# NSA's values and window keys projected beside the stick-breaking values in a two-layer decoder trunk

## The chip, the cores and the metric

The kernel runs on one core of one Trainium2 chip. The metric is the device time of one execution in microseconds. Five engines work on their own in-order queues: TensorE (PE, matmuls, with its weight load PEld), VectorE (DVE), ScalarE (ACT), GpSimd (POOL) and SyncE (SP), which issues nearly all transfers here.

## The reference

Two layers over 512 tokens of width 1024. Each layer normalises its input, projects it once with `w_in`, feeds five attention branches from the columns of that product, gates and merges their outputs, projects them and adds the residual:

```python
h = _rmsnorm(x, norm_g)
p = _split_columns(h @ w_in)
...
y_a = _dsa_attention(q_a, k_a, v_a, qi, ki, p['idx_w'])        # A: top-128 keys by an indexer
y_b = _fox_attention(...)                                      # B: forgetting attention
y_c = _stick_breaking_attention(heads(p['sb_q']), heads(p['sb_k']), heads(p['sb_v']))
y_d = _nsa_attention(q_d, _rope(p['nsa_kc'], positions), p['nsa_vc'],
                     _rope(p['nsa_ks'], positions), p['nsa_vs'],
                     _rope(p['nsa_kw'], positions), p['nsa_vw'], gates, ...)
y_e = _memory_attention(heads(p['mem_q']), mem_k, mem_v)       # E: 256 memory tokens
...
merged = jnp.sum(merge * jnp.einsum('bsnc,ncd->bsnd', ys, w_branch), axis=2)
return x + merged @ w_out
```

Each branch has four heads of 64. NSA (branch D) has one 64-wide key and value per token, shared by the heads, for each of three parts: compressed (`kc`, `vc`), selected blocks (`ks`, `vs`) and the local window (`kw`, `vw`). Keys are rotated (`_rope`), values are not. The indexer of branch A picks 128 keys for every query: `lax.top_k(score, 128)`.

## The kernel before

**Products.** Every float32 product is made of three matmuls. Each operand is split in a rounded part (`hi`) and the rest (`lo`), and hi x hi, hi x lo and lo x hi are summed in a PSUM bank (`mm3`, line 264). Weights come in half chunks of 128 x 1024 (512 KB, `load`, line 277): SyncE issues the transfer into `wraw` (two buffers), ScalarE copies it to `whi` (line 271), VectorE subtracts to get `wlo` (line 272); three buffers each. `proj` (line 520) then makes 128 columns of `h @ w_in` for all 512 tokens: eight k tiles of 128 times three matmuls, 24 matmuls of 128x512 into a bank named `pj`. Such an output has its columns on partitions (channel-major). Banks come from three pools: `pj` (3), `S` (2), `T` (3). Intermediate 128x512 tiles come from one pool of `NST` slots.

**The chunks concerned.** `PAIRS` puts two such projections in one weight chunk. Half `('k1', 0)` holds `nsa_kc` and `nsa_ks`; its other half `k2` holds `nsa_kw` in 64 columns and nothing in the others; the second half of `ckv`'s chunk, `v1`, holds `nsa_vs` and `nsa_vw`.

**First stage of a layer** (`first`, from line 711). It works on `u = x * g`, before the norm factor is known, so that it can start early. It projects queries and keys of the first stick-breaking pair (banks `p`), sums squares, and gets the norm factor `y` of each token (`rs_y` in the profile). Then it forms the stick-breaking values for all tokens, token-major: the x tiles are the stationary operand, 256 weight columns move, 4 token blocks x 8 k tiles x 3 = 96 matmuls of 128x256. After two token blocks, `rowb` spreads `y` over the partitions as `rb` (line 364). ScalarE evacuates the values with the factor `y` into `VC` (line 780). `norm` (line 785) forms `hr = x * g * rb` (line 791) and its parts `h_hi`, `h_lo`, on which every later projection waits.

**The later stages of a layer** are built by `weave` (line 675), which draws from several generators in turn by weights; `chain` puts generators behind each other, `take(g, n)` draws only n steps of one. The stages: `sb_attn(0)` (first stick-breaking pair) with side projections; `sb_attn(1)` with more projections and the first two steps of `nsa_proj`; the memory stage, `mem_attn` with `merge(2)`, the rest of `nsa_proj` and 18 steps of `topk`; the NSA stage, `nsa_attn` with `merge(4)`, `dsa_proj` and the rest of `topk`; then DSA, FoX and the last merges, and the output projection. The text drawn so is not the order on the chip: a scheduler places every instruction on its engine's queue by priority and by its own estimate of when inputs are ready. Weight loads and splits get a high priority (`early`).

**nsa_proj** (from line 1090): `k1` is projected and rotated, its upper half becomes the selected keys `KS`; `k2` is projected, rotated and becomes the window keys `KW` (`shared_k`, line 498, writes a key to both halves of a tile with its low part); `v1` is projected, copied out (`vraw`), turned to token-major by four transposes into the bank `vt` (line 1137) and copied to `VSW` (line 1139), whose columns 0-63 of a block are selected values and 64-127 window values.

**topk** (from line 930 on): 16 rounds for each of three blocks of queries (256, 384 and 512 keys wide): VectorE finds the 8 largest (`MAX8`, line 933) and replaces them (`MATCH_REPLACE8`, line 934). 48 such block rounds per layer; each is one step of the generator. Three comparisons (line 937) then make the masks, which only `dsa_attn` reads.

Of the kernel before, what the change touches and what calls it, by code (L numbers as in the profile page):

```python
# [28 lines left out]
NST = 28  # L29
# [18 lines left out]
def _tiles():  # L48
# [19 lines left out]
    k2 = -np.ones(128, int)  # L68
    k2[0:64] = c('nsa_kw', a(64))
    t['k2'] = k2  # L70
    t['v1'] = np.concatenate([c('nsa_vs', a(64)), c('nsa_vw', a(64))])
# [10 lines left out]
PAIRS = [('v2', 'iq'), ('k1', 'k2')]  # L82
PAIRS += [(('sb_q', 0), ('sb_k', 0)), (('sb_q', 1), ('sb_k', 1))]
PAIRS += [('ckv', 'v1'), (('dsa_q', 0), ('dsa_q', 1)), (('nsa_q', 0), ('nsa_q', 1))]
# [3 lines left out]
VTOK = ['sb_v', 'fox_v']  # L88
# [5 lines left out]
for _n in ['memk', 'memv', 'wc1k', 'wc1v'] + [f'wb{n}' for n in range(5)] + [f'wo{n}' for n in range(4)]:  # L94
    CH[_n] = len(CH)
# [8 lines left out]
def _layout(x, mem, positions, norm_g, w_in, kv_norm, w_uk, w_uv, fox_bias, nsa_pe_k, nsa_pe_v,  # L104
# [6 lines left out]
    for l in range(L):  # L111
# [75 lines left out]
def trunk(ctx: ExitStack, tc: tile.TileContext, xt, memt, pos, wall, small, vec, ca, cb, out):  # L187
# [89 lines left out]
    def load(l, key, half):  # L277
        with early():
            r = wts.tile([128, 1024], F32, name="wraw", tag="raw", bufs=2)
            nc.sync.dma_start(r, wall[l, CH[key], :, 1024 * half:1024 * half + 1024])  # L280
        return r

    def wload(l, key, half, r=None):
        r = load(l, key, half) if r is None else r
        with early():
            hi = wts.tile([128, 1024], F32R, name="whi", tag="whi", bufs=3)
            lo = wts.tile([128, 1024], F32R, name="wlo", tag="wlo", bufs=3)
# [420 lines left out]
    def layer(l, xs, begin):  # L708
# [3 lines left out]
        def first():  # L712
# [32 lines left out]
            w = []  # L745
            for half in range(2):
                if l:
                    w.append(wload(l, 'sb_v', half))
                else:
                    r = load(l, 'sb_v', half)  # L750
                    w.append([wts.tile([128, 1024], F32R, name="w", tag=t, bufs=3) for t in ("whi", "wlo")])
                    after(nc.scalar.activation(w[half][0], r, AF.Copy), state['start'][0])
                    after(nc.vector.tensor_sub(w[half][1], r, f32(w[half][0])), state['start'][1])
            lv.VC = wk.tile([128, NB, 256], F32, name="VC", tag="v", bufs=1)
            vb = []
# [16 lines left out]
            yield  # L772
            lv.QC += q_stack(qr)
# [4 lines left out]
            for t in range(2):  # L778
                for e in range(2):
                    nc.scalar.activation(lv.VC[:, 2 * t + e], vb[t][:, e], AF.Copy, scale=y[:, 2 * t + e:2 * t + e + 1])  # L780
# [309 lines left out]
        def nsa_proj():  # L1090
            kr = rope(pj('k1'))
# [374 lines left out]
```

## Time and profile before

| what | value |
|---|---|
| median of 3 runs | 1329.06 us (1328.14 to 1329.29) |
| the profiled execution | 1328.6 us, its span 1326.8 us |
| granted TensorE clock, mean | 0.998 |
| instructions | 18877 |
| busiest engine | PE 1297.0 us, 98% of the span |
| next | DVE 913.9 us, 69%; ACT 677.2 us, 51% |

The span is the time from the first to the last instruction; the execution is 1.8 us longer. The busy time of an engine is the time in which one of its instructions is under way; since matmuls are pipelined, one's duration is longer than the distance to the next. The lines of groups read: line, engine, operation, output<-inputs by tile name, shapes, count, then busy us and mean ns of one, then the idle time just before them and what ended it. In a timeline: start, duration, engine, line, operation, output<-inputs, shapes. In layer 0 the first stage ends at about 36 us, `sb_attn(0)` at 100, `sb_attn(1)` at 162, the memory stage at 255 and the NSA stage near 380.

### The profile page before, as it was taken

To read this page: it belongs to the slowest core of one execution; us is meant where nothing else is said; L and a number is where in the kernel's file an instruction comes from. 1 tells how busy PE (TensorE), PEld (TensorE's weight loads), DVE (VectorE), ACT (ScalarE), POOL (GpSimd) and SP (SyncE) were. 2 spreads that over 40 slices of the span, in tenths; PEclk is the share of its full clock that TensorE was granted. 3 is DMA by queue.
4 is the path that set the end of the run, shared out by engine and by line. 5 is a ranking of instruction groups with operands and counts; after the bars stand their busy time and mean duration, and the time that the engine had idled before them with its cause. 6 is when DMAs were issued, how large, how long until landed. Compare 5 with 4: busy or idle time off the path is not lost.

```text
span 1326.8 us, 18877 instructions
## 1 busy us (share of the span) xinstructions
PE 1297.0 (98%) x7160; PEld 1063.6 (80%) x7160; DVE 913.9 (69%) x1966; ACT 677.2 (51%) x1265; POOL 41.8 (3%) x60
## 2 busy tenths in 40 slices
PE   7999999999999999999999999999999999999997
PEld 6777777888788888888887777877878878888897
DVE  6887999777755556554667699996686564574554
ACT  6887835356544434333447696534584443342341
POOL 0000011000000000000000001110000000000000
PEclk9999999999999999999999999999999999999999
DMA  6432232222213221233623323223122222223231
GB/s 223 137 127 73 90 108 64 82 78 75 72 64 103 67 92 58 70 104 125 192 88 127 96 64 128 80 64 95 49 88 64 79 88 70 91 79 112 96 112 64
DMA packets 40235, 124.10 MB, mean 94 GB/s; under 512 B 4432, under 2 KB 6480, under 8 KB 40144
## 3 DMA queue, kind: packets, MB, share of 16 engines
q1 hardware_dynamic: 40144, 122.89, 28.5%
q8 instruction: 56, 0.92, 0.3%
q14 instruction: 35, 0.29, 0.1%
HBM read 118.16 MB, written 4.72 MB: 93 GB/s over the span
## 4 chain that ended last, share of the span: by engine, by line
PE 70%; DVE 6%; ACT 5%; issue 2%; DMA 1%; POOL 0%; DVEq 0%; ACTq 0%
PE pj L261 59%; PE Y L261 4%; PE S L261 3%; PE pt L573 3%; ACT whi L271 1%; DVE wlo L272 1%; DVE score L934 1%; DVE m L933 1%; ACT sw L448 1%; ACT sw L447 1%; DMA mraw<-in_memt_dram 1%; PE sbz L261 0%; ACT sp_t L405 0%; ACT Qi L877 0%; DVE rt L450 0%
## 5 line engine op out<-in xcount | busy, mean ns | idle before, releaser
L261 PE MATMUL pj<-h_hi,whi 128*128 128x512 f32 x1088 | 431.2, 398 | 1.3 <-DVE rt L450 1.0
L261 PE MATMUL pj<-h_lo,whi 128*128 128x512 f32 x1088 | 428.5, 394 | 0.0
L261 PE MATMUL pj<-h_hi,wlo 128*128 128x512 f32 x1088 | 428.3, 394 | 0.0
L271 ACT ACTIVATE whi<-wraw 128x1024 fp32r<-128x1024 f32 x183 | 193.4, 1057 | 333.0 <-PE pj L261 173.7
L272 DVE TENSOR_TENSOR wlo<-wraw,whi 128x1024 fp32r<-128x1024 f32 x183 | 223.6, 1222 | 185.7 <-ACT whi L271 167.2
L261 PEld LDWEIGHTS pj<-h_hi,wlo 128*128 128x128 f32 x1088 | 204.3, 188 | 46.4 <-DVE wlo L272 3.1
L261 PEld LDWEIGHTS pj<-h_hi,whi 128*128 128x128 f32 x1088 | 204.5, 188 | 42.7 <-DVE rt L450 1.8
L261 PEld LDWEIGHTS pj<-h_lo,whi 128*128 128x128 f32 x1088 | 204.6, 188 | 41.3 <-issue 2.6
L564 ACT ACTIVATE P<-P,nm 128x128 f32<-128x128 f32 (+3 forms) x128 | 71.5, 559 | 77.7 <-DVE nm L563 77.0
L261 PE MATMUL pj<-yhi,whi 128*128 128x512 f32 (+1 forms) x192 | 72.5, 378 | 1.3 <-ACT whi L271 0.5
L563 DVE CUSTOM_DVE_ANT_0 P<-S,CA 128x128 f32<-128x128 f32 (+3 forms) x104 | 48.5, 470 | 35.9 <-PE S L261 35.7
L261 PE MATMUL pj<-ylo,whi 128*128 128x512 f32 (+1 forms) x192 | 71.8, 374 | 0.0
L261 PE MATMUL pj<-yhi,wlo 128*128 128x512 f32 (+1 forms) x192 | 71.7, 374 | 0.0
L573 PE MATMUL pt<-CA,P 128*128 128x128 f32 x384 | 60.2, 274 | 1.7 <-DVE P L612 1.4
L573 PEld LDWEIGHTS pt<-CA,P 128*128 128x128 f32 x384 | 45.6, 141 | 13.0 <-issue 5.0
L411 ACT ACTIVATE G<-pj 128x512 f32<-128x512 f32 x92 | 53.7, 583 | 1.9 <-PE pj L261 1.7
L934 DVE MATCH_REPLACE8 score<-m,score 128x256 f32<-128x256 f32 (+2 forms) x96 | 51.6, 541 | 0.0
L261 PE MATMUL S<-Ks,Qs 128*128 128x256 f32 (+2 forms) x160 | 49.3, 347 | 0.9 <-DVE nm L563 0.9
L933 DVE MAX8 m<-score 128x8 f32<-128x256 f32 (+2 forms) x96 | 49.8, 547 | 0.0
L828 DVE SCALAR_TENSOR_TENSOR G<-G,pj 128x512 f32<-128x512 f32 x64 | 43.6, 681 | 1.3 <-PE pj L261 0.8
L829 DVE TENSOR_TENSOR acc<-acc,G 128x512 f32<-128x512 f32 x64 | 44.0, 687 | 0.7
L261 PEld LDWEIGHTS pj<-yhi,whi 128*128 128x128 f32 x192 | 36.1, 188 | 9.2 <-ACT yhi L271 1.3
(333 smaller groups left out, 2028.2 us busy)
## 6 DMA issues: line engine op xcount, KB each, us to landing
wraw<-in_wall_dram SPq DMA_DIRECT2D x192, 512.0 KB, 3.7
wc<-in_wall_dram SPq DMA_DIRECT2D x16, 256.0 KB, 5.9
x<-in_xt_dram SPq DMA_DIRECT2D x8, 256.0 KB, 5.8
mraw<-in_memt_dram SPq DMA_DIRECT2D x4, 512.0 KB, 4.5
xo<-in_xt_dram SPq DMA_DIRECT2D x8, 256.0 KB, 3.9
xspill<-xn SPq DMA_DIRECT2D x8, 256.0 KB, 2.2
xo<-xspill SPq DMA_DIRECT2D x8, 256.0 KB, 3.0
out_dram<-o SPq DMA_DIRECT2D x8, 256.0 KB, 2.2
```

Source lines behind the costliest of these rows:

```text
L261: return nc.tensor.matmul(out_, lhsT, rhs, start=start, stop=stop, **kw)
L271: nc.scalar.activation(hi, raw, AF.Copy)
L272: nc.vector.tensor_sub(lo, raw, hi.bitcast(F32))
L411: i = nc.scalar.activation(*a, **k)
L447: nc.scalar.activation(sw[a], p[b], AF.Copy)
L563: nc.vector.tensor_tensor_reduce(P, S, mask, -1.0, 3e38, OP.add, OP.min, nm)
L564: nc.scalar.activation(P, P, AF.Exp, bias=nm, scale=-1.0, accum_out=sums)
L573: nc.tensor.transpose(pt[:, 128 * j:128 * j + 128], x[:, c:c + 128], ident)
L828: nc.vector.scalar_tensor_tensor(G, G, gc, p, op0=gop, op1=OP.mult)
L829: nc.vector.tensor_add(acc, acc, G)
L933: nc.vector.max(m8, lv.work[i])
L934: nc.vector.match_replace(lv.work[i], m8, lv.work[i], REPL)
```

## The change

The 192 columns of `nsa_vs`, `nsa_vw` and `nsa_kw` move beside the 256 of the stick-breaking values. The first stage now forms all 448 columns token-major: 96 matmuls of 128x448 in place of 96 of 128x256, from four half chunks of 128x896 (`vt0`, `vt1`) in place of two of 128x1024. The loops are turned: the k tile is outside, the token block inside, so four banks (one of `pj`, both of `S`, one of `T`) are open at once and `rowb` comes after half of the k tiles. `VC` takes 256 columns, a new tile `VK` the other 192, both times `y`. NSA's attention reads its values from `VK` as they lie. The window keys need columns on partitions: a new function `window_keys`, drawn at the end of the side chain of `sb_attn(0)`, transposes columns 64 to 191 of `VK` (four transposes into the bank `kwT`), rotates them and makes `KW`. The projections of `k2` and `v1`, `vraw`, the transposes `vt` and `VSW` are gone; `k1` shares a chunk with `ckv`. Besides, the weave draws 14 block rounds of the top-k in the memory stage, not 18, the weight of the rest in the NSA stage is 40, not 36, the side chain's weight in `sb_attn(0)` is 11, not 10, and `NST` is 27, not 28.

```diff
-NST = 28
+NST = 27
...
-    t['v1'] = np.concatenate([c('nsa_vs', a(64)), c('nsa_vw', a(64))])
+    t['vt'] = np.concatenate([c('sb_v', a(256)), c('nsa_vs', a(64)), c('nsa_vw', a(64)), c('nsa_kw', a(64))])
...
-PAIRS = [('v2', 'iq'), ('k1', 'k2')]
+PAIRS = [('v2', 'iq'), ('ckv', 'k1')]
...
-            w = []
-            for half in range(2):
+            v = [bank("v", t)[:, :448] for t in ("pj", "S", "S", "T")]
+            for i in range(KT // 2):
                 if l:
-                    w.append(wload(l, 'sb_v', half))
+                    hi, lo = wload(l, f'vt{i // 2}', i % 2, n=896)
...
-            for t in range(0, NB, 2):
-                v = bank("pj", "S", (128, 2, 256))
-                last = None
-                for e in range(2):
-                    for k in range(KT):
-                        hi, lo = w[k // 4]
-                        c = slice(256 * (k % 4), 256 * (k % 4) + 256)
-                        ts = slice(128 * (t + e), 128 * (t + e) + 128)
-                        for a_, b_ in ((uh, hi), (ul, hi), (uh, lo)):
-                            last = acc_mm(v[:, e], a_[k][:, ts], b_[:, c], last)
-                vb.append(v)
-                if t == 0:
+                for k in (2 * i, 2 * i + 1):
+                    c = slice(448 * (k % 2), 448 * (k % 2) + 448)
+                    for t in range(NB):
+                        ts = slice(128 * t, 128 * t + 128)
+                        mm(v[t], uh[k][:, ts], hi[:, c], k == 0, False)
+                        mm(v[t], ul[k][:, ts], hi[:, c], False, False)
+                        mm(v[t], uh[k][:, ts], lo[:, c], False, k == KT - 1)
+                if i == 1:
                     lv.rb = rows_sb(rowb(y, 4), T, "rb")
...
+            for t in range(NB):
+                nc.scalar.activation(lv.VC[:, t], v[t][:, 0:256], AF.Copy, scale=y[:, t:t + 1])
+                nc.vector.tensor_scalar(lv.VK[:, t], v[t][:, 256:448], y[:, t:t + 1], None, op0=OP.mult)
...
-            kr = rope(pj('k1'))
+            kr = rope(pj('ckv', 1))
...
-            lv.KW = shared_k(rope(pj('k1', 1)), lower)
-            yield
-            p = pj('ckv', 1)
-            vraw = slot("vraw")
-            nc.scalar.activation(vraw, p, AF.Copy)
...
-            pt = bank("vt", "T")
-            for j in range(NB):
-                nc.tensor.transpose(pt[:, 128 * j:128 * j + 128], vraw[:, 128 * j:128 * j + 128], ident)
-            lv.VSW = slot("VSW")
-            nc.vector.tensor_copy(lv.VSW, pt)
...
+        def window_keys():
+
+            pt = bank("kwT", "pj")
+            for t in range(NB):
+                nc.tensor.transpose(pt[:, 128 * t:128 * t + 128], lv.VK[:, t, 64:192], ident)
+            lv.KW = shared_k(rope(pt), upper)
+            yield
+
...
-                              lambda h, j, vo_=vo_: lv.VSW[:, 128 * j + vo_:128 * j + vo_ + 64], lv.gt[:, i, 4 + 4 * b:8 + 4 * b])
+                              lambda h, j, vo_=vo_: lv.VK[:, j, vo_:vo_ + 64], lv.gt[:, i, 4 + 4 * b:8 + 4 * b])
...
-        weave((mem_attn(), 8), (merge(2, lv.YC, first=True), 8), (chain(nsa, silu2('nsa_z', lv.ZD)), 13), (take(tk, 18), 18))
-        weave((nsa_attn(), 32), (merge(4, lv.YE, halves=True), 16), (dsa_proj(), 9), (tk, 36))
+        weave((mem_attn(), 8), (merge(2, lv.YC, first=True), 8), (chain(nsa, silu2('nsa_z', lv.ZD)), 13), (take(tk, 14), 14))
+        weave((nsa_attn(), 32), (merge(4, lv.YE, halves=True), 16), (dsa_proj(), 9), (tk, 40))
```

Two places show how the scheduler's order moves. The first is ScalarE's queue where layer 0 goes from the values to the projections of `h`; `VC` is the evacuation of the values, `rb` the spread norm factor, `h_hi` the rounded parts of `h`, `Qs` a piece of the first queries. Before:

```order
L364 ACTIVATE rb<-rowb 128x512
L780 ACTIVATE VC<-pj,rs_y 128x256
L417 ACT_TABLE_LOAD
L271 ACTIVATE h_hi<-hr 128x512
L271 ACTIVATE whi<-wraw 128x1024
...
L780 ACTIVATE VC<-pj,rs_y 128x256 x2
L271 ACTIVATE h_hi<-hr 128x512 x3
L482 ACTIVATE Qs<-qr 64x512
```

Now, from `rb` on:

```order
L364 ACTIVATE rb<-rowb 128x512
L271 ACTIVATE h_hi<-hr 128x512 x2
L271 ACTIVATE whi<-wraw 128x1024
L271 ACTIVATE h_hi<-hr 128x512
L770 ACTIVATE VC<-v,rs_y 128x256 x2
L271 ACTIVATE h_hi<-hr 128x512 x2
L271 ACTIVATE whi<-wraw 128x1024
L271 ACTIVATE h_hi<-hr 128x512
L770 ACTIVATE VC<-v,rs_y 128x256 x2
L482 ACTIVATE Qs<-qr 64x512
L271 ACTIVATE h_hi<-hr 128x512 x2
```

All four `VC` now stand among the `h_hi`, two ahead of the fourth and two ahead of the last two. Before, one stood ahead of `rb` (not shown), one behind it, and two ahead of the fourth `h_hi`.

The second is VectorE's queue at the end of layer 0's memory stage; `score` are the blocks of the top-k, `m` their maxima, `y<-Y,Z` is the fourth and last output block of the memory attention, and the rows behind it (`P,nm`) begin the NSA stage. Before:

```order
L934 MATCH_REPLACE score_1229<-m_3604,score_1229 128x384
L647 RECIPROCAL rsum<-rsum 128x2
L933 MAX m_3640<-score_1230 128x8
L937 TENSOR_SCALAR score_1228<-score_1228 128x256
L934 MATCH_REPLACE score_1230<-m_3640,score_1230 128x512
L937 TENSOR_SCALAR score_1229<-score_1229 128x384
...
L272 TENSOR_TENSOR wlo<-wraw,whi 128x1024
L665 TENSOR_TENSOR y<-Y,Z 128x256
L563 ISA P,nm<-S,CA 128x128
```

Now:

```order
L930 MATCH_REPLACE score_1267<-m_3520,score_1267 128x256
L929 MAX m_3590<-score_1268 128x8
L929 MAX m_3632<-score_1269 128x8
L930 MATCH_REPLACE score_1268<-m_3590,score_1268 128x384
L930 MATCH_REPLACE score_1269<-m_3632,score_1269 128x512
L933 TENSOR_SCALAR score_1267<-score_1267 128x256
...
L272 TENSOR_TENSOR wlo<-wraw,whi 128x1024
L665 TENSOR_TENSOR y<-Y,Z 128x256
L563 ISA P,nm<-S,CA 128x128
```

In both orders the last block round and the three comparisons stand ahead of the stage's last `y`, so every round lies before the NSA stage; of the 48 block rounds, 43 lie between the end of the second stick-breaking pair and that `y` before, and 46 now.

More of the change, by code (lines that the diff above doesn't have):

```diff
@@ L275, in split, with load, wload @@
             nc.vector.scalar_tensor_tensor(lo, raw, scale, hi.bitcast(F32), op0=OP.mult, op1=OP.subtract)
-    def load(l, key, half):
+    def load(l, key, half, n=1024):
         with early():
-            r = wts.tile([128, 1024], F32, name="wraw", tag="raw", bufs=2)
-            nc.sync.dma_start(r, wall[l, CH[key], :, 1024 * half:1024 * half + 1024])
-        return r
-    def wload(l, key, half, r=None):
-        r = load(l, key, half) if r is None else r
+            r = wts.tile([128, 1024], F32, name="wraw", tag="raw", bufs=2)[:, :n]
+            nc.sync.dma_start(r, wall[l, CH[key], :, 1024 * half:1024 * half + n])
+        return r
+    def wload(l, key, half, r=None, n=1024):
+        r = load(l, key, half, n) if r is None else r
         with early():
-            hi = wts.tile([128, 1024], F32R, name="whi", tag="whi", bufs=3)
-            lo = wts.tile([128, 1024], F32R, name="wlo", tag="wlo", bufs=3)
+            hi = wts.tile([128, 1024], F32R, name="whi", tag="whi", bufs=3)[:, :n]
+            lo = wts.tile([128, 1024], F32R, name="wlo", tag="wlo", bufs=3)[:, :n]
             split(r, hi, lo)
@@ L744, in first @@
                 run(tabg)
-            w = []
-            for half in range(2):
+            v = [bank("v", t)[:, :448] for t in ("pj", "S", "S", "T")]
+            for i in range(KT // 2):
                 if l:
-                    w.append(wload(l, 'sb_v', half))
+                    hi, lo = wload(l, f'vt{i // 2}', i % 2, n=896)
                 else:
[L750 to L755, printed above, removed]
-            for t in range(0, NB, 2):
-                v = bank("pj", "S", (128, 2, 256))
-                last = None
-                for e in range(2):
-                    for k in range(KT):
-                        hi, lo = w[k // 4]
-                        c = slice(256 * (k % 4), 256 * (k % 4) + 256)
-                        ts = slice(128 * (t + e), 128 * (t + e) + 128)
-                        for a_, b_ in ((uh, hi), (ul, hi), (uh, lo)):
-                            last = acc_mm(v[:, e], a_[k][:, ts], b_[:, c], last)
-                vb.append(v)
-                if t == 0:
+                    r = load(l, f'vt{i // 2}', i % 2, 896)
+                    hi, lo = (wts.tile([128, 1024], F32R, name="w", tag=t, bufs=3)[:, :896] for t in ("whi", "wlo"))
+                    after(nc.scalar.activation(hi, r, AF.Copy), state['start'][0])
+                    after(nc.vector.tensor_sub(lo, r, f32(hi)), state['start'][1])
+                for k in (2 * i, 2 * i + 1):
[6 more added lines that the diff above has]
+                if i == 1:
                     lv.rb = rows_sb(rowb(y, 4), T, "rb")
@@ L1414, in layer @@
             ln_phase()
-            weave((sb_attn(0), 8), (chain(silu2('sb_z', lv.ZC), take(ixp, 1), take(sp1, 1), take(ixp, 1), mp), 10))
+            weave((sb_attn(0), 8), (chain(silu2('sb_z', lv.ZC), take(ixp, 1), take(sp1, 1), take(ixp, 1), mp, window_keys()), 11))
         else:
@@ L1418, in layer @@
             ln_phase()
-            weave((sb_attn(0), 8), (chain(silu2('sb_z', lv.ZC), take(ixp, 1), take(sp1, 1), take(ixp, 1), mp), 10))
+            weave((sb_attn(0), 8), (chain(silu2('sb_z', lv.ZC), take(ixp, 1), take(sp1, 1), take(ixp, 1), mp, window_keys()), 11))
         tk = topk()
```

20 lines of the change are left out of this document (8 added, 12 removed).

## The prediction

> **What bounds the kernel now.** I read the page first: the busy line, the slices of the span and the chain that ended last.
>
> ```profile
> span 1326.8 us, 18877 instructions
> PE 1297.0 (98%) x7160; PEld 1063.6 (80%) x7160; DVE 913.9 (69%) x1966; ACT 677.2 (51%) x1265; POOL 41.8 (3%) x60
> PE   7999999999999999999999999999999999999997
> PE 70%; DVE 6%; ACT 5%; issue 2%; DMA 1%; POOL 0%; DVEq 0%; ACTq 0%
> ```
>
> TensorE is busy in nine tenths or more of every slice but the first and the last, and holds 70% of the chain. Next, TensorE's waits (what it waited for; us in total, times, longest):
>
> ```profile
> PE pj L261 <- ACT w L728: 8.7, 1, 8.7
> PE sbz L261 <- DVE sp_t L990: 2.5, 5, 1.0
> PE pj L261 <- ACT whi L271: 0.5, 1, 0.5
> PE pj L261 <- DVE wlo L272: 0.3, 1, 0.3
> ```
>
> Only the start is a wait of any size, and the change leaves it alone. A matmul taken away is therefore time taken away, as long as the other engines deliver as early as now. Whether they can is seen in the windows of layer 0: the second stick-breaking stage, the memory stage, the NSA stage. Columns after the length: TensorE, weight load, VectorE, ScalarE, GpSimd (busy us and counts), clock, DMA share, GB/s.
>
> ```profile
> 100.00:162.00 62.00, 60.89 (x292) 46.53 (x289) 52.99 (x99) 49.59 (x93) 1.83 (x2) 1.00 0.22 70
> 162.00:255.00 93.00, 92.02 (x528) 73.03 (x527) 89.86 (x225) 38.85 (x76) 14.30 (x16) 1.00 0.28 92
> 255.00:380.00 125.00, 123.93 (x725) 100.76 (x724) 85.84 (x221) 68.40 (x141) 1.04 (x2) 1.00 0.24 76
> ```
>
> In the memory stage VectorE is busy 89.86 of 93.00 us, almost as full as TensorE. That is the place to watch.
>
> **What a matmul costs.** Durations in the profile overlap, so the price is the distance between starts. TensorE's timeline in layer 1's first stage, and one pair of 384 columns in layer 0:
>
> ```profile
> 59.23 0.51 PE L261 MATMUL sbz<-Qs,Ks 128*128 128x384 f32 x2
> 59.58 0.39 PE L261 MATMUL pj<-h_hi,whi 128*128 128x512 f32 x1
> ...
> 668.37 0.39 PE L261 MATMUL pj<-u,whi 128*128 128x512 f32 x1
> ...
> 673.59 0.39 PE L261 MATMUL pj<-u,wlo 128*128 128x512 f32 x1
> ...
> 677.04 0.28 PE L261 MATMUL pj<-whi,u 128*128 128x256 f32 x1
> ...
> 679.92 0.28 PE L261 MATMUL pj<-whi,u 128*128 128x256 f32 x1
> ```
>
> From 668.37 to 673.59 lie 23 steps of 512 columns: 5.22 / 23 = 0.227 us. From 677.04 to 679.92 lie 24 steps of 256: 2.88 / 24 = 0.120. The two of 384 take 59.58 - 59.23 = 0.35, so 0.175 each. No row has 448 columns; its price lies between 0.175 and 0.227. The three prices stand on a line (0.120 to 0.175 to 0.227), so I take 0.175 + 0.052 / 2 = 0.201.
>
> **Matmuls removed and added, both layers.** Four half chunks are not projected any more (two per layer, 24 matmuls of 512 each): 96 x 0.227 = -21.8 us. The 96 value matmuls per layer grow from 256 to 448 columns: 192 x (0.201 - 0.120) = +15.6; by the bounds 192 x 0.055 = +10.6 and 192 x 0.107 = +20.5. The eight transposes of `vt` go and eight of `kwT` come, of one shape, so nothing. TensorE's sum: -21.8 + 15.6 = **-6.2 us** (bounds -11.2 and -1.3). This assumes that distance between starts is the cost. [...]
>
> **Where they leave and where they come.** Per layer the first stage gains 96 x 0.081 = 7.8 us; the side work behind it moves up, so the first attention stage gets one half chunk more (+24 x 0.227 = 5.4), the second one two fewer (-10.9), the memory stage one fewer (-5.4) and the transposes (-0.4). The later stages hold the same instructions as before.
>
> **The first stage.** The groups that feed chunks, and the chunk's DMA:
>
> ```profile
> L271 ACT ACTIVATE whi<-wraw 128x1024 fp32r<-128x1024 f32 x183 | 193.4, 1057 | 333.0 <-PE pj L261 173.7
> L272 DVE TENSOR_TENSOR wlo<-wraw,whi 128x1024 fp32r<-128x1024 f32 x183 | 223.6, 1222 | 185.7 <-ACT whi L271 167.2
> wraw<-in_wall_dram SPq DMA_DIRECT2D x192, 512.0 KB, 3.7
> ```
>
> Each new chunk of 896 columns feeds 24 matmuls, 24 x 0.201 = 4.8 us. Its load, copy and subtract take at most 3.7, 1.06 and 1.22 us on three different engines, so four chunks in place of two are hidden; uncovered, one would cost 6 us. Evacuating 192 more columns costs VectorE four instructions no longer than the 0.42 of a 128x256 one (quoted below), off TensorE's path.
>
> What isn't hidden is an order of waiting. Layer 0 around the handover, ScalarE, VectorE and TensorE:
>
> ```profile
> 35.72 0.40 PE L261 MATMUL pj<-h_hi,whi 128*128 128x512 f32 x1
> ...
> 37.31 0.81 ACT L780 ACTIVATE VC<-pj,rs_y 128x256 f32<-128x256 f32 x2
> ...
> 42.73 1.41 DVE L791 SCALAR_TENSOR_TENSOR hr<-x,VEC,rb 128x512 f32<-128x512 f32 x2
> ...
> 43.51 1.29 ACT L271 ACTIVATE h_hi<-hr 128x512 fp32r<-128x512 f32 x2 [1.31 <-DVE hr L791]
> ...
> 44.88 1.29 DVE L272 TENSOR_TENSOR h_lo<-hr,h_hi 128x512 fp32r<-128x512 f32 x2
> ...
> 46.90 0.31 PE L261 MATMUL sbz<-Qs,Ks 128*128 128x256 f32 x1
> ```
>
> Now TensorE goes from values to projections without loss: 50 matmuls between 35.72 and 46.90, 0.224 each. With k outside, all four banks end in the last k tile, at -1.8, -1.2, -0.6 and 0 us (12 x 0.201 = 2.4 us). In ScalarE's new order two `VC` copies stand ahead of the fourth and fifth `h_hi`. They wait for the first two banks and end at -0.8 (0.41 each), those `h_hi` at 0.4 (0.6 each). Behind come a chunk's copy (1.5), the sixth `h_hi` (2.1), two `VC`, a Q copy, and the last two `h_hi` (4.1, 4.7). VectorE follows: fifth `h_lo` 1.0, a `wlo` 2.2, sixth `h_lo` 2.8, two `hr` 4.1, two `VK` 4.8, seventh `h_lo` 5.4. TensorE, at 3 x 0.227 = 0.68 us per k tile, wants the seventh `h_lo` at 6 x 0.68 + 0.23 = 4.3. It waits 1.1 us per layer, **+2.2** in all; 0 if everything starts a little earlier (0 is what the same place costs now), +4.4 if the lateness is double.
>
> **The memory stage.** The rounds of the top-k, the removed copy, and how late things come there:
>
> ```profile
> L934 DVE MATCH_REPLACE8 score<-m,score 128x256 f32<-128x256 f32 (+2 forms) x96 | 51.6, 541 | 0.0
> L933 DVE MAX8 m<-score 128x8 f32<-128x256 f32 (+2 forms) x96 | 49.8, 547 | 0.0
> ...
> 140.71 0.42 DVE L933 MAX8 m<-score 128x8 f32<-128x256 f32 x1
> ...
> 193.95 0.68 DVE L1139 COPY VSW<-vt 128x512 f32<-128x512 f32 x1
> ...
> 198.50 1.22 DVE L272 TENSOR_TENSOR wlo<-wraw,whi 128x1024 fp32r<-128x1024 f32 x1
> ...
> 247.96 0.68 DVE L933 MAX8 m<-score 128x8 f32<-128x512 f32 x1
> ...
> 254.62 0.42 DVE L665 TENSOR_TENSOR y<-Y,Z 128x256 f32<-128x256 f32 x1
> ...
> 203.94 0.40 PE L261 MATMUL pj<-h_hi,wlo 128*128 128x512 f32 x1
> ```
>
> Rounds run from 140.71 to 247.96 and end before the stage's last `y` at 254.62. The new numbers (14 instead of 18, then 40 instead of 36) are meant to put fewer of them here. In VectorE's order they don't: before, 5 block rounds stand in the second stick-breaking stage and 43 in the memory stage; now 2 and 46. A generator's `take` limits what may be drawn, and the order fills VectorE with rounds wherever it is free. So VectorE gets three block rounds more, 3 x (0.547 + 0.541) = +3.3, and loses a `wlo` (-1.2), `VSW` (-0.7) and a small reduction (-0.4): about +1.0, to 90.9 us. TensorE's own work falls from 92.0 to 86.2. VectorE is then 4.7 us longer than TensorE. Its lead is what covers that: the chunk whose `wlo` starts at 198.50 and lasts 1.22 is read by TensorE at 203.94, 4.2 us after it is ready, the shortest lead of a chunk that I found there. 4.7 - 4.2 = 0.5 per layer stay uncovered, **+1.0** for both layers; nothing if VectorE runs further ahead, 2 x 4.7 = +9.4 if no lead counts.
>
> **Sum.** -6.2 + 2.2 + 1.0 = **-3.0 us** on the profiled execution's 1328.6, so 1325.6; that execution lies 0.46 under the median of the runs, 1329.06, so the forecast is **1326.0 us**. Without the two losses it would be 1329.06 - 6.2 = 1322.9.
>
> **Rivals.**
>
> *The cover holds whole* (the `h` tiles are in time, VectorE's lead is enough): 1322.9, down to 1318 if 448 columns cost 0.175. For it: TensorE waits for VectorE nowhere over 1.0 us now. Against it: the two orders worked out above. Faster.
>
> *448 columns cost what 512 cost.* TensorE saves only 1.3 us, the time is 1327.8 with no losses and 1331.0 with both. Against it: 384 columns cost 0.175, less than 512. Same.
>
> *VectorE sets the pace of the memory stage.* Place: its queue between 162 and 255 us and the same place of layer 1. With no lead, TensorE gives back 9.4 there: -6.2 + 2.2 + 9.4 = +5.4, 1334.5, slower. It decides once the lag passes 4.2 us by more than 1.6 per layer (then the sum is above zero). For it: 89.86 of 93.00 busy already, rounds not moved out. Against it: after 255 VectorE is busy 85.84 of 125.00, so a lag is soon made up, and TensorE has merges to run that need only old chunks. [...]
>
> *The edit of the rounds does nothing.* By the order that is so; it is in the forecast.
>
> **How the numbers follow.** The forecast with the losses roughly as sized (1324.5 to 1327.5) 0.44, the cover holding 0.24, the 512 price 0.10, VectorE's pace 0.22, of which the slower part (over 1331.7) 0.13 and the rest between 1327.5 and 1331.7. Range 1319.5 to 1332.0: it leaves out the cheapest 448 price and the far end of VectorE's pace. A measurement of this kernel tells 0.2%, 2.7 us, from no change: faster is under 1326.4, slower over 1331.7. Of the forecast's 0.44, 0.30 lie under 1326.4. Faster 0.30 + 0.24 = 0.54, slower 0.13, same 0.33.
>
> **What would show it.** Starts of `v` matmuls 0.20 us apart confirm the first term. A wait of TensorE for `h_lo` or `h_hi` of 1 to 2 us in each layer's first projection confirms the second. In the memory stage, waits of TensorE for `wlo` or `PT` that are not there now, and VectorE without a gap over 85 to 91 us, confirm the third; rounds in the NSA stage would refute the reading of the order. The prediction is wrong if the memory stage keeps its 93 us, or if the first stage grows by more than 12 us.

## The result, and the profile after

The changed kernel takes 1343.96 us (median; 1341.86 to 1346.1) where the kernel before took 1328.71 beside it: the ratio is 1.0113, with a 95% interval of 1.0101 to 1.0125. It is slower by 15 us, outside the range. The profiled execution took 1341.86 us at a mean granted clock of 0.994; the executions near 1346 show 0.990, the kernel before 0.998. One execution of a later kernel (e15) took 1420.61 us at a clock of 0.85 throughout and is left out of its numbers. The head of the changed kernel's page:

```profile
span 1340.1 us, 18712 instructions
PE 1299.0 (97%) x7064; PEld 1059.6 (79%) x7064; DVE 915.2 (68%) x1972; ACT 675.1 (50%) x1263; POOL 41.7 (3%) x60
PE 78%; DVE 10%; ACT 8%; issue 2%; DMA 2%; POOL 0%; SPq 0%; DVEq 0%; ACTq 0%; POOLq 0%
```

TensorE has 96 matmuls fewer, as planned, and yet is busy 2 us longer, in a span that is 13.3 us longer. On the chain that ended last VectorE went from 6% to 10% and ScalarE from 5% to 8%, with about the same work on each. TensorE's longest waits in total, beside the one at the start and one of 2.6 us for ScalarE's `PT` (what for; us in total, times, longest):

```profile
PE sbz L261 <- DVE sp_t L982: 4.7, 6, 2.4
PE sbz L261 <- DVE sp L998: 2.5, 2, 1.3
PE S L261 <- ACT P L1285: 2.0, 2, 1.0
```

The new waits are for the stick-breaking softplus (`sp_t`, `sp`) and for memory attention's first probabilities (`P`, L1285). None is for `h_lo`, `wlo` or a top-k round.

**The sum of the work.** Thirteen steps of 448 columns in layer 1's first stage, and layer 0's first matmul on `h`:

```profile
43.54 0.40 PE L261 MATMUL pj<-h_hi,whi 128*128 128x512 f32 x1
...
697.12 0.37 PE L261 MATMUL v<-whi,ul 128*128 128x448 f32 x1
...
699.81 0.37 PE L261 MATMUL v<-wlo,u 128*128 128x448 f32 x1
```

2.69 / 13 = 0.207 us a step, so the values cost 192 x 0.087 = 16.7 us more and TensorE's sum is -21.8 + 16.7 = -5.1. The first `h` matmul moved from 35.72 to 43.54: 7.8 us later, as forecast. If matmuls alone counted, the span would be 5.1 us shorter; it is 13.3 longer, so TensorE waits or is slowed for 18.4 us more. Adding up, over TensorE's whole timeline, what each distance between starts has beyond the usual spacing of its shape gives about the same, 18 us more than before.

**Where.** The last VectorE row of each of layer 0's first stages: the two stick-breaking stages end with `yC`, the memory stage with `y`. Before (its memory stage ended at 254.62):

```profile
100.67 0.69 DVE L1031 TENSOR_TENSOR yC<-Yc,Z 128x512 f32<-128x512 f32 x1 [1.70 <-PE Yc L261]
...
161.71 0.69 DVE L1031 TENSOR_TENSOR yC<-Yc,Z 128x512 f32<-128x512 f32 x1
```

After:

```profile
114.48 0.69 DVE L1023 TENSOR_TENSOR yC<-Yc,Z 128x512 f32<-128x512 f32 x1 [1.94 <-PE Yc L261]
...
164.61 0.69 DVE L1023 TENSOR_TENSOR yC<-Yc,Z 128x512 f32<-128x512 f32 x1 [1.72 <-PE Yc L261]
...
257.95 0.42 DVE L665 TENSOR_TENSOR y<-Y,Z 128x256 f32<-128x256 f32 x1
```

The same rows of layer 1 start at 753.98, 812.46 and 906.56 before and at 772.75, 823.30 and 919.03 after. From these starts, with the forecast of the prediction's placement step:

| per layer | forecast | layer 0 | layer 1 |
|---|---|---|---|
| second stick-breaking stage | -10.9 | 61.0 to 50.1: -10.9 | 58.5 to 50.6: -7.9 |
| memory stage | -5.8 | 92.9 to 93.3: +0.4 | 94.1 to 95.7: +1.6 |

The stages that gain matmuls grew about as planned. The stages that lose them gave back 10.5 and 6.3 us where 16.7 were due in each layer. But the work did not leave where the forecast had it. Counted between these rows in TensorE's timelines, the 512-column matmuls on `h` fell from 181 to 112 and from 170 to 114 in the second stick-breaking stage (69 and 56, which is 15.7 and 12.7 us), and from 272 to 269 and from 280 to 277 in the memory stage. So the memory stage kept its time because it kept its matmuls, and the -10.9 of layer 0, equal to the forecast, is a coincidence: 15.7 us of work left, and 4.8 us of waiting and slow clock came in its place. In layer 1 it is the same 4.8. The windows of layer 0 there, after (TensorE, weight load, VectorE, ScalarE, GpSimd, clock, DMA share, GB/s):

```profile
154.00:160.00 6.00, 3.17 (x14) 1.81 (x12) 5.70 (x11) 5.90 (x12) 0.00 (x0) 1.00 0.50 138
160.00:164.00 4.00, 4.00 (x14) 1.62 (x16) 2.88 (x9) 3.48 (x8) 1.23 (x2) 0.57 1.01 270
164.00:172.00 8.00, 6.43 (x74) 4.39 (x71) 6.64 (x18) 2.56 (x7) 2.78 (x3) 1.00 0.25 92
172.00:258.00 86.00, 85.55 (x453) 67.71 (x452) 83.97 (x213) 34.78 (x65) 11.75 (x14) 1.00 0.22 70
```

In layer 0 the loss is not spread over the memory stage: from 172 to 258 TensorE is busy 85.55 of 86.00. It lies in 18 us around the handover. From 154 to 160 TensorE is busy 3.17 of 6.00 while ScalarE (5.90) and VectorE (5.70) are full; then its clock falls to 0.57 for 4 us; then it idles another 1.57. The same stretch before:

```profile
154.00:160.00 6.00, 5.50 (x31) 4.21 (x28) 6.00 (x16) 4.82 (x10) 0.22 (x1) 1.00 0.05 15
160.00:164.00 4.00, 3.90 (x21) 3.06 (x20) 3.97 (x8) 2.56 (x6) 1.61 (x2) 1.00 0.86 223
164.00:172.00 8.00, 8.00 (x44) 6.03 (x46) 7.63 (x21) 2.49 (x6) 1.83 (x2) 1.00 0.71 272
```

What TensorE lacked from 154 is seen in its own timeline, after:

```profile
154.45 0.40 PE L261 MATMUL pj<-yhi,wlo 128*128 128x512 f32 x1
155.69 0.38 PE L261 MATMUL S<-KE,Qs 128*128 128x256 f32 x1 [0.85 <-ACT sb_a L405]
...
158.51 0.50 PE L261 MATMUL sbz<-sp,ntri 128*128 128x512 f32 x1 [0.59 <-DVE sp L999]
160.00 0.39 PE L261 MATMUL S<-KE,Qs 128*128 128x256 f32 x1 [0.99 <-ACT P L1285]
```

and in ScalarE's, whose last stick-breaking exponential (`sb_a`) is followed by the table load of the next phase and the first gate `G` of `merge(2)`:

```profile
159.85 0.59 ACT L405 ACTIVATE sb_a<-sbz 128x512 f32<-128x512 f32 x1
160.46 1.28 ACT L422 ACT_TABLE_LOAD   x1
161.75 0.60 ACT L411 ACTIVATE G<-pj 128x512 f32<-128x512 f32 x1
```

The last matmul of the side work starts at 154.45 (it is the first half of a product of `merge(2)`), and the last exponential comes at 159.85. For those 5.4 us the only matmuls left are those of the stick-breaking chain itself and the first scores of memory attention, most of them waiting for ScalarE or VectorE. The merges did not step in: the other half of that product needs this stage's own `yC` and starts at 166.02, and the first gate is evaluated behind the table load. Before, ScalarE's rows read:

```profile
151.49 0.57 ACT L405 ACTIVATE sb_a<-sbz 128x512 f32<-128x512 f32 x1
152.08 1.28 ACT L422 ACT_TABLE_LOAD   x1
...
163.93 0.58 ACT L1110 ACTIVATE vraw<-pj 128x512 f32<-128x512 f32 x1
```

and in TensorE's timeline projections on `h` ran on:

```profile
156.83 0.50 PE L261 MATMUL pj<-h_hi,whi 128*128 128x512 f32 x1 [0.51 <-DVE rt L450]
...
162.18 0.39 PE L261 MATMUL pj<-h_hi,wlo 128*128 128x512 f32 x1
```

They end 10.7 us past the start of that exponential. That surplus lay over the end of the chain; the stage lost more than it, 15.7 us. The 24 matmuls from 156.83 to 162.18 are, by their place in the generator and by the copy `vraw` that follows them, the projection `v1`: drawn in the memory stage, counted there by the prediction, and placed by the scheduler ahead of it, where they filled the end of the stick-breaking chain. The chain did get shorter without the projections (the last exponential starts 45.4 us after the previous `yC`, before 50.8), but by much less than the matmuls. Layer 1 shows the same after its second stick-breaking stage, in the changed kernel:

```profile
816.00:820.00 4.00, 2.41 (x11) 0.98 (x11) 3.70 (x10) 3.91 (x8) 0.00 (x0) 0.92 0.90 288
820.00:824.00 4.00, 4.00 (x23) 2.12 (x20) 2.27 (x8) 2.31 (x8) 1.83 (x2) 0.65 0.92 318
```

### The profile page after: what moved, and what is told of

It is laid out like the page before. It is cut to its first block, busy times and chain, and to the rows that moved or that the text cites. A ratio compares the mean times of both kernels' runs of the same rounds, so it can differ in the third digit from the quotient of the medians.

```text
span 1340.1 us, 18712 instructions
## 1 busy us (share of the span) xinstructions
PE 1299.0 (97%) x7064; PEld 1059.6 (79%) x7064; DVE 915.2 (68%) x1972; ACT 675.1 (50%) x1263; POOL 41.7 (3%) x60
## 4 chain that ended last, share of the span: by engine, by line
PE 78%; DVE 10%; ACT 8%; issue 2%; DMA 2%; POOL 0%; SPq 0%; DVEq 0%; ACTq 0%; POOLq 0%
PE pj L261 62%; PE Y L261 4%; PE S L261 3%; PE v L261 3%; PE pt L573 3%; ACT whi L271 2%; DVE wlo L272 1%; DVE score L930 1%; DVE m L929 1%; DMA wraw<-in_wall_dram 1%; PE Yc L261 1%; PE sbz L261 1%; ACT sw L447 1%; ACT sw L448 1%; ACT Qi L873 1%
## 5 line engine op out<-in xcount | busy, mean ns | idle before, releaser
L261 PE MATMUL pj<-h_hi,whi 128*128 128x512 f32 x1056 | 420.6, 399 | 0.1
L261 PE MATMUL pj<-h_hi,wlo 128*128 128x512 f32 x1056 | 416.2, 394 | 0.0
L261 PE MATMUL pj<-h_lo,whi 128*128 128x512 f32 x1056 | 414.9, 393 | 0.0
L271 ACT ACTIVATE whi<-wraw 128x1024 fp32r<-128x1024 f32 (+1 forms) x181 | 191.0, 1056 | 345.2 <-PE pj L261 189.3
L272 DVE TENSOR_TENSOR wlo<-wraw,whi 128x1024 fp32r<-128x1024 f32 (+1 forms) x181 | 220.5, 1219 | 202.9 <-ACT whi L271 184.3
L261 PEld LDWEIGHTS pj<-h_hi,wlo 128*128 128x128 f32 x1056 | 198.6, 188 | 46.0 <-DVE wlo L272 3.5
L261 PEld LDWEIGHTS pj<-h_hi,whi 128*128 128x128 f32 x1056 | 199.0, 188 | 40.1 <-issue 2.4
L261 PEld LDWEIGHTS pj<-h_lo,whi 128*128 128x128 f32 x1056 | 199.0, 188 | 38.8 <-issue 2.0
```

Of the source, the lines that this page charges most:

```text
L261: return nc.tensor.matmul(out_, lhsT, rhs, start=start, stop=stop, **kw)
L271: nc.scalar.activation(hi, raw, AF.Copy)
L272: nc.vector.tensor_sub(lo, raw, hi.bitcast(F32))
```

## The experiments

Four theories. **A**, lost cover: the end of the second stick-breaking stage goes by its chain on ScalarE and VectorE; projections taken from it leave TensorE bare there and in the handover, and the clock falls behind (above to 0.57). **B**, the prediction's rival: VectorE's queue sets the pace of the memory stage. **C**: the small edits (slots, weight of the side chain, rounds) make the loss. **D**, formed later: layer 1's memory tokens arrive late, behind the longer row of loads.

**Which part of the change.** First the changed kernel with the small edits undone (label e1, on the changed kernel), then the small edits alone (e2, on the kernel before):

```diff
-NST = 27
+NST = 28
-... mp, window_keys()), 11))
+... mp, window_keys()), 10))
-... (take(tk, 14), 14))
+... (take(tk, 18), 18))
-... (tk, 40))
+... (tk, 36))
```

> The changed kernel with the small edits undone: top-k draws 18 and weight 36, side chain weight 10, 28 slots. Theory A (lost cover: the second stick-breaking stage is as long as its ScalarE and VectorE chain; two half chunks fewer leave TensorE bare at its end, and its clock falls there): about 1342, like the changed kernel, with TensorE bare for some 5 us ahead of the second stage's last product in both layers. Theory B (VectorE's queue sets the pace of the memory stage): about 1342 too, since all rounds stay where they are. Theory C (the small edits make the loss): 1326 to 1330.

> The kernel before with the small edits alone: top-k draws 14 and weight 40, side chain weight 11, 27 slots. A and B: within 1327 to 1331. C: 1338 to 1344.

Measured: e1 1342.04 us (1341.4 to 1345.97), ratio 1.0105 [1.0089, 1.0121]; e2 1334.22 (1333.25 to 1335.1), 1.0039 [1.0024, 1.0054]. With the edits undone the loss is still there, so C does not carry it. But e2 is a miss for all: alone, these edits cost 5.4 us. Where that lies in layer 0, in e2:

```profile
84.00:88.00 4.00, 2.31 (x15) 1.66 (x14) 3.68 (x7) 3.49 (x9) 0.00 (x0) 1.00 0.39 131
88.00:92.00 4.00, 3.59 (x17) 2.96 (x17) 3.21 (x6) 2.62 (x7) 0.00 (x0) 0.64 0.29 84
```

A stretch that is half bare, then four microseconds at 0.64: the same pattern, in the first stick-breaking stage. In layer 1's, TensorE waits 2.66 us for a softplus tile at 735, and the clock is at 0.50 from 734 to 741. The weight of the side chain alone (e19, on the kernel before) was tried for it:

```diff
-... mp), 10))
+... mp), 11))
```

> The kernel before with the side chain's weight in the first stick-breaking stage at 11 instead of 10, nothing else. In the orders of all engines the new top-k numbers move four instructions of VectorE and none of another engine, the slot count eight rows of TensorE, the weight 97. If the weight makes the loss of the small edits (TensorE bare once in each first stick-breaking stage, clock halved after it): 1333 to 1335. If the slot count does: 1328 to 1330.

Measured 1330.65 (1329.23 to 1332.83), 1.0016 [1.0007, 1.0025]: below what was expected if it were the weight, some 2 of the 5.4. How the rest divides between the slots and their combination with the weight wasn't settled.

**VectorE's pace.** e4 keeps 2 of the 16 rounds of the top-k (6 of the block rounds in the memory stage); it leaves out 14 rounds of each block, so its masks differ.

```diff
-            for r in range(16):
+            for r in range(2):
-... (take(tk, 14), 14))
+... (take(tk, 6), 6))
```

> The changed kernel with 2 rounds of the top-k in place of 16 (the selection of branch A is then of other keys: 42 of 48 block rounds per layer left out, 46 us of VectorE's work per layer, most of it in the memory stage). Theory A: the bare time lies where almost no rounds stand: 1339 to 1344. Theory B: the memory stage gets back what it lost, 5 us or more per layer: 1326 to 1334.

Measured 1343.9 us (1342.27 to 1344.72), 1.0109 [1.0094, 1.0124]. The memory stage of e4:

```profile
172.00:258.00 86.00, 85.58 (x451) 67.65 (x450) 45.44 (x90) 34.57 (x64) 12.12 (x13) 1.00 0.22 72
```

VectorE's busy time there fell from 83.97 to 45.44, and neither TensorE's row nor the time of the kernel moved. B is refuted: VectorE was full because it had rounds to fill in, not because TensorE waited for it.

**Cover, given back.** e3 adds, in each layer, two projections that nobody reads at the end of the second stage's side chain, 24 matmuls of 512 columns each (21.8 us in all, work that the reference doesn't have):

```diff
-... take(nsa, 2)), 12))
+... take(nsa, 2), filler(2)), 12))
```

> The changed kernel with two dummy projections per layer (24 matmuls of 128x512 each, made of h alone, no weights, only eight columns of the result copied) drawn at the end of the second stick-breaking stage's side chain: 96 matmuls, 21.8 us of TensorE work that the result does not need. A: they fall into time that is lost anyway: 1338 to 1347, and the granted clock stays at 1.00 at the end of that stage. B and C: 1342 + 22 = 1364.

Measured 1351.09 (1350.39 to 1351.5), 1.0168 [1.0151, 1.0184]: 4 us above the upper end that A gave, 13 below what B and C gave. Of 21.8 us added, 7 show. The clock stays at 1.00 from 154 to 164, and TensorE is busy 5.79 of 6.00 in the former gap. So two thirds of the filler cost no time; a fall of the clock in layer 1, near 731, stayed (the mean over the span is 0.996, 0.998 before).

Useful work in its place: e5 draws the first projection of `dsa_proj`, e7 makes the first NSA query projection before the compression matmuls at the head of the memory stage, e8 makes both, the first of them in the second stick-breaking stage. The core of e5, then of e7 (e8 moves the second projection as well and draws `take(nsa, 3)`):

```diff
-... take(nsa, 2)), 12))
+... take(nsa, 2), take(dp, 1)), 12))
```

```diff
             yield
+            qr = [rope(pj(('nsa_q', 0)))]
+            lv.QD = q_stack(qr[0])
+            yield
 
             ht = sm.tile([128, 128], F32, name="ht", bufs=1)
...
-            qr = [rope(pj(('nsa_q', 0)))]
-            lv.QD = q_stack(qr[0])
-            yield
```

> The changed kernel with the first step of the DSA projections (one half chunk, 24 matmuls, one copy and one square on ScalarE) drawn in the second stick-breaking stage and no more in the NSA stage; no work added or left out. A: the bare time of about 8.7 us per layer (with the slow clock) shrinks by 5 to 8 us: 1327 to 1333. B and C: 1342, since neither the memory stage's VectorE work nor the small edits change.

> The changed kernel with one step of NSA's side chain moved: the first query projection (24 matmuls of h) stands ahead of the compression matmuls, so that it is the first work of the memory stage. Nothing is added or left out. Theory A (TensorE bare from the end of the second stick-breaking stage to the start of the memory stage, and its clock halved behind that): the 5.4 us of matmuls cover part of it in both layers: 1331 to 1338. Theory B (VectorE's queue paces the memory stage): 1342 to 1344, since VectorE's work is the same.

> The changed kernel with both query projections of NSA ahead of the compression matmuls, the first drawn in the second stick-breaking stage, the second first in the memory stage: they take the places that the two dropped half chunks had. Nothing is added or left out. Theory A: the waits of the second stick-breaking and the memory stage fall back to those of before, about 12 us less than in the changed kernel: 1328 to 1333, the clock dips at the end of the second stage gone in both layers. Theory B: 1342 to 1344.

Measured: e5 1337.11 (1335.65 to 1338.04), 1.006 [1.0045, 1.0075], the right direction but 4 short; e7 1333.66 (1332.43 to 1335.72), 1.0036 [1.0023, 1.0049], as A had it; e8 1335.51 (1334.54 to 1337.12), 1.0049 [1.0034, 1.0064], 2.5 above its range. So a move of one projection, with no matmul added or removed, takes back 10 of the 15 us. e7 at the place:

```profile
154.00:160.00 6.00, 5.91 (x29) 4.67 (x27) 5.69 (x12) 5.92 (x12) 0.00 (x0) 1.00 0.31 91
160.00:164.00 4.00, 3.84 (x23) 2.34 (x24) 4.00 (x11) 2.19 (x5) 1.29 (x2) 1.00 0.00 0
164.00:172.00 8.00, 8.00 (x44) 6.03 (x43) 7.97 (x20) 5.52 (x11) 1.36 (x2) 1.00 0.49 135
```

ScalarE and VectorE are as full as in the changed kernel, TensorE has its cover again, and the clock stays at 1.00. e5 covers the end of the stage alone; in it TensorE is bare from 164 to 168 (1.36 of 4.00) and at 0.50 from 168 to 172. The handover needs cover too.

e11 is e8 with the small edits undone.

> As the kernel with both query projections early, with the small edits undone too (18 and 36 for the top-k, side chain weight 10, 28 slots). Theory A with the loss of the small edits seen alone (5 us, from bare TensorE in the first stick-breaking stage): 1322 to 1328, faster than both kernels. If the small edits cost nothing beside the new values: as the kernel with both queries early.

Measured 1331.01 (1329.65 to 1332.25), 1.0016 [1.0006, 1.0025]: 4.5 us under e8, and 3 above the range. What was left was a fall of the clock near 720, in layer 1's first stick-breaking stage: behind a wait of 2.71 us for `sp_t` (to 720.65), seven steps of 512 columns take 725.18 - 722.19 = 2.99 us, 0.427 each.

**Layer 1's memory tokens.** The changed kernel has it too. VectorE there (`mraw`: raw memory tokens, scaled on arrival), then TensorE:

```profile
722.29 0.88 DVE L1241 SCALAR_TENSOR_TENSOR mraw<-mraw,VEC,rmem 128x256 f32<-128x256 f32 x2 [6.30 <-DMA mraw<-in_memt_dram]
...
725.62 0.42 DVE L982 SCALAR_TENSOR_TENSOR sp_t<-sbz,sp_t 128x256 f32<-128x256 f32 x1
```

```profile
723.42 0.23 PE L261 MATMUL sbz<-sbm,identb 128*128 128x128 bf16 x1
726.09 0.51 PE L261 MATMUL sbz<-sp,nones 128*128 128x256 f32 x2 [2.43 <-DVE sp_t L982]
```

VectorE stands 6.30 us for a transfer at the head of its queue; the softplus tile `sp_t` is queued behind, and TensorE waits 2.43 us for it. SyncE's queue, before, then after:

```profile
702.93 0.33 SPq L1248 DMA_DIRECT2D mraw<-in_memt_dram  x1
703.35 0.55 SPq L842 DMA_DIRECT2D cosI<-rot  x1
```

```profile
710.80 0.55 SPq L838 DMA_DIRECT2D cosI<-rot  x1
713.89 0.33 SPq L1238 DMA_DIRECT2D mraw<-in_memt_dram  x1
```

Before, the first transfer of the tokens goes out ahead of the rotary tables, 4.4 us before VectorE scales it at 707.31; now it goes out behind them, 11 us later, and VectorE, which has reached it at 716, starts on it 8.4 us after the issue. Waits for this tile are not new (VectorE stood 2.98 us for the second transfer before), but in the changed kernel they come to 6.7 us, and one of them now stops TensorE. That is D. Why the transfer goes out late is seen in the kernel and in SyncE's waits: `mraw` uses the same two buffers as `wraw`, and from 690 to 735 SyncE waits 11.3 us, 9.4 of them at one time, for VectorE to be done with a weight chunk (`wlo`) before it can load the tokens. e16 puts the tokens at the start of the side chain (with a step of its own for load and scaling), on the changed kernel; e14 does the same on e11:

```diff
-... chain(silu2('sb_z', lv.ZC), take(ixp, 1), ...
+... chain(take(mp, 1), silu2('sb_z', lv.ZC), take(ixp, 1), ...
```

> The changed kernel with one thing moved: in layer 1's first stick-breaking stage the memory tokens are loaded and scaled at the start of the side chain, ahead of the two rotary loads on SyncE's queue, not behind them. Nothing is added or left out. Theory D (VectorE stands 6 us behind the late memory tokens in layer 1, TensorE waits 2.4 us for the softplus tile queued behind them, and its clock is halved after that): 1336 to 1340, no clock dip near 725 us. If the late tokens do not matter: 1342 to 1344.

> Both query projections early, the small edits undone, and the memory tokens of layer 1 loaded at the start of its side chain. Theories A and D together: 1331 less 3 to 5: 1326 to 1328, no clock dip between the start and the final norm. If D falls: 1331.

Measured: e16 1349.15 (1348.17 to 1350.19), 1.0156 [1.0141, 1.0172]; e14 1335.07 (1334.14 to 1336.12), 1.005 [1.0038, 1.0063]. Both slower than what they start from, by 5 and 4 us. e16 around the place:

```profile
708.00:712.00 4.00, 1.35 (x9) 0.89 (x9) 3.75 (x11) 3.42 (x9) 0.00 (x0) 0.82 0.00 0
712.00:716.00 4.00, 2.15 (x5) 1.17 (x5) 3.60 (x11) 4.00 (x12) 0.00 (x0) 0.50 0.11 12
```

With the tokens first, the `sb_z` projections come later, and the head of the stage lies bare instead: another loss of cover, larger than the wait it cured. SyncE's waits from 694 to 716 in e16 show why the projections are late:

```profile
SPq L280 <- DVE ylo L272: 19.8, 1, 19.8
```

The tokens hold both weight buffers until VectorE has split them, and no weight chunk goes out between 694 and 714. As a test of D these two runs tell nothing; they test A again. e15 therefore puts the tokens behind the `sb_z` projections, still ahead of the rotary loads, on e11; e17 does so with e7's placing of the queries, small edits undone:

```diff
-... chain(silu2('sb_z', lv.ZC), take(ixp, 1), ...
+... chain(silu2('sb_z', lv.ZC), take(mp, 1), take(ixp, 1), ...
```

> As the kernel before it, the memory tokens of layer 1 behind the two gate projections of the side chain instead of ahead of them; still ahead of the rotary loads. A and D: 1326 to 1328. If D falls: 1331.

> The changed kernel with the small edits undone, the first query projection of NSA ahead of the compression matmuls at the head of the memory stage, and layer 1's memory tokens loaded ahead of the rotary loads, behind the gate projections. Theories A and D: like the kernel with both queries early and the tokens second, 1327 to 1330, faster than before only if the bare time of its second stage is shorter; if covering with one projection is not enough: 1331 to 1335.

Measured: e15 1329.24 us (1327.25 to 1330.54), 1.0002 [0.9993, 1.0011]; e17 1327.75 (1326.07 to 1330.06), 0.9993 [0.9984, 1.0002]. From 716 to 732 e15 and the changed kernel read:

```profile
716.00:732.00 16.00, 15.46 (x70) 12.27 (x71) 9.71 (x17) 9.94 (x18) 0.00 (x0) 1.00 0.42 134
```

```profile
716.00:732.00 16.00, 13.25 (x55) 10.48 (x54) 9.18 (x23) 8.89 (x22) 0.00 (x0) 0.89 0.34 107
```

70 matmuls at full clock instead of 55 at 0.89. e15 is 1.8 us under e11, 1.2 above the upper end of D's expectation and 1.8 below the time expected if D falls; its clock is 0.998 over the span, as in the kernel before. e17 is 16 us under the changed kernel and can't be told from the kernel before. Between e17 and the changed kernel lie cover, tokens and small edits together. With them put back the whole loss is gone, while the 5.1 us of matmuls saved show as nothing that can be measured. Where they went in e17 can be read: TensorE idles 31.9 us of the span (29.8 before), and one fall of the clock (0.59 from 714 to 718) costs 1.6; the span is 1.3 us shorter. TensorE idles less than before in the second stick-breaking stages (0.66 and 0.67 us against 1.11 and 1.12) and more in the memory stages (1.99 and 2.64 against 0.98 and 0.56).

**The clock by itself.** The clock theory of these experiments is that the falls of the granted clock seen so far come from TensorE's own waits: in the changed kernel it was at 0.50 from 728 to 730, behind the wait of 2.43 us that ended at 726.09. Two kernels on the one before make TensorE wait between the fourth and fifth product of layer 0's output projection, a place with nothing else to run: 2 copies of a tile on VectorE (e20) or 6 (e21), then a transpose that needs them. The copies are work that the reference doesn't have:

```diff
+                if l == 0 and m == 4:
+                    d = slot("gapd")
+                    nc.vector.tensor_copy(d, p)
+                    for _ in range(6 - 1):
+                        nc.vector.tensor_copy(d, d)
...
+                    i0 = nc.tensor.transpose(p[:, 0:128], d[:, 0:128], ident)
```

> The kernel before with TensorE made to wait once, in layer 0's output projection, where it otherwise never waits: two VectorE copies of 128x512 in a row (0.6 us each) and one transpose stand between the fourth and the fifth of its products. [...]

> The same with six VectorE copies: a gap of about 4 us. Clock theory: granted clock near 0.5 for 3 to 4 us after the gap, matmuls of 128x512 at 0.43 us a step in it, and a loss of the gap and 1.5 to 2 us more: 1334 to 1336. If the dips seen near the other waits had another cause: the gap alone, clock 1.00: 1332 to 1333.

Measured: e20 1334.51 (1334.03 to 1335.56), 1.0043 [1.0028, 1.0058]; e21 1337.09 (1336.89 to 1338.45), 1.0064 [1.0048, 1.0081]. The gap of e20, which was meant to be 1.5 us with no fall behind it and a time of 1330 to 1331, came out at 4.56 us, and the clock fell there too: 0.62 from 644 to 648, 0.96 from 648 to 652. e21 behind its gap, TensorE's timeline and two windows:

```profile
640.38 0.39 PE L261 MATMUL pj<-g_hi,wlo 128*128 128x512 f32 x1
647.18 0.47 PE L1341 MATMUL pj<-CA,gapd 128*128 128x128 f32 x1 [6.40 <-DVE gapd L1339]
...
648.30 0.63 PE L261 MATMUL pj<-g_hi,wlo 128*128 128x512 f32 x1
...
651.29 0.63 PE L261 MATMUL pj<-g_hi,whi 128*128 128x512 f32 x1
```

```profile
648.00:652.00 4.00, 4.00 (x11) 3.13 (x10) 0.00 (x0) 0.00 (x0) 0.00 (x0) 0.50 0.02 4
652.00:656.00 4.00, 4.00 (x19) 3.26 (x19) 0.69 (x1) 0.92 (x1) 0.00 (x0) 1.00 0.00 0
```

Seven steps of 512 columns take 651.29 - 648.30 = 2.99 us, 0.427 each instead of 0.227, and by 652 it is over (1.00 in the next window). The span grew by 8.6 us, of which 6.6 are the gap; the remaining 2.0 are put down to the slow matmuls behind it (1.4 in e20). So in both the gap was paid for, and then 1.4 and 2.0 us more.

## Why the prediction was wrong

The step that failed is the placement: "the second one two fewer (-10.9), the memory stage one fewer (-5.4)", taken as time under the sentence "A matmul taken away is therefore time taken away, as long as the other engines deliver as early as now". It failed twice. The work left elsewhere: 69 and 56 matmuls went from the second stick-breaking stage (15.7 and 12.7 us) and 3 from the memory stage, since `v1`, drawn in the memory stage, ran ahead of it. And it was not time: the condition was examined for the first stage and for VectorE in the memory stage, and not for the stage that loses most. At its end ScalarE and VectorE work through their chain and the projections only filled TensorE beside it, for 10.7 us; with 15.7 us gone TensorE stands (busy 3.17 of 6.00 us) and its clock falls (to 0.57). The second stage gave back 4.8 us less than its lost matmuls in both layers. The sign that the prediction named, a memory stage that keeps its 93 us, came (93.3 and 95.7), but not by the VectorE lead that it was meant to test.

- **448 columns, 0.201 us.** Right in kind, mis-sized: 0.207, so the sum of work is -5.1 instead of -6.2.
- **The first stage grows by 7.8 per layer.** Right: the first `h` matmul moved by 7.8.
- **h_lo late, +2.2.** Not there. From 43.54 the `h` projections run at their 0.227 in layer 0; no wait for `h_hi` or `h_lo` is in the list.
- **The rounds don't move out of the memory stage.** Right, and e4 shows that it doesn't matter.
- **VectorE's lead in the memory stage, +1.0, and its rival at 1334.5.** Both refuted by e4; the rival that ended on the slower side had the wrong mechanism. Two slips there change nothing: by the prediction's own sum the rival decides from 2.0 us per layer, not 1.6, and TensorE did wait once more than 1.0 us for VectorE (1.3, for `rs_y`).
- **Not in the sum:** the end of the second stick-breaking stage and its handover. Layer 0, from the windows, idle time and clock against before: (2.83 - 0.50) idle in 154 to 160, 4.00 x 0.43 = 1.7 of clock, 1.57 idle in 164 to 172, together 5.6 us. Layer 1's handover by the same reckoning (808 to 832 after against 804 to 820 before) is 3.85 idle and 1.7 of clock less 0.59, together 5.0. e3, e5, e7 and e8 show the cause.
- **Not in the sum:** layer 1's token load. From 702 to 754 before and from 711 to 773 after, its first stick-breaking stage, TensorE idles 2.31 and 4.42 us, and 16.00 x 0.11 = 1.8 of clock come from 716 to 732: 3.9 us. e11 against e15 shows 1.8 us of the token wait as time.

These make 14.5 of the 18.4 us. By the heads of the two pages TensorE idles 29.8 us before and 41.1 after, 11.3 more, and the three falls of the clock cost 1.7, 1.7 and 1.8: 16.5. So some 2 us more are idle time elsewhere, part of it in the rest of layer 1's memory stage; the last 2 weren't located. In e17, whose matmuls are 5.1 us shorter and which ends where the kernel before does, 2.1 us more idle time and one fall of the clock account for nearly all that is missing. Why its memory stages idle more wasn't tested.

The signs were in the trace of before. The prediction read its window of 62 us as one row: TensorE 60.89, VectorE 52.99, ScalarE 49.59, which looks like 9 us of slack on the others. Cut into 6 us, its end shows VectorE at 6.00 of 6.00 and ScalarE at 4.82; and `sb_a`'s last row at 151.49 beside the last projection at 162.18 gives the slack directly, 10.7 us. Half of it was `v1`, as `vraw`'s row shows. By the prediction's own prices this one stage was therefore to lose 16.3 us, its 10.9 and `v1`'s 5.4.

## What to carry to other kernels

Before counting removed matmuls as time, ask in each stage which engine's chain ends it and by how much the matmuls that can run beside it outlast that chain: only that surplus is to be had, and a stage that loses more needs other independent matmuls moved in (here one projection of the next stage took back 10 of 15 us). Count in the timeline, not in the program's text, in which stage the removed matmuls ran (here `v1` was drawn in one stage and ran in the one before). Look at the end of a stage in windows of a few microseconds, because shares over the whole stage hide it. And follow each small load whose buffers the change keeps busy longer (here the tokens wait for the weights' two): the late tile at the head of VectorE's queue held VectorE for 6.30 us here, and TensorE for 2.43 us by way of the softplus tile queued behind it.

## What the hardware showed that was not expected

The granted clock fell to about half behind some of TensorE's waits, and in these runs not by the length of the gap alone. It fell at gaps of 6.40 us (e21; 0.50 from 648 to 652) and 4.56 us (e20; 0.62 from 644 to 648), but also at a single gap of 2.43 us (to 726.09, after; 0.50 from 728 to 730), at one of 1.34 us (713, e17; TensorE busy 0.85 of 2.00 from 712 to 714, the clock 0.59 from 714 to 718) and behind 6 us in which TensorE was busy 3.17 with no gap over 0.99 (154 to 160, after; 0.50 from 160.6 to 164.0). Gaps of 1.85 us (836, e15) and 1.92 us (828, e17) had no fall behind them; the next windows show 1.00. A fall lasted 3.4 us (after, 160.6 to 164.0) or twice that (e21, 645.1 to 652.0); beside the gap it cost 1.4 us in e20 and 2.0 in e21. In e21's fall a step of 512 columns took 0.427 us, and 0.227 outside falls. What makes the clock fall after one stretch and not after another was not shown.
